# A four-layer encoder on one core: the last combination of each down group split in parts, other work moved behind its neighbours

## The chip, the cores and the metric

The kernel runs on one core of a Trainium2 chip. The metric is the device time of one execution in microseconds (us). The core has five engines that run their own queues of instructions: TensorE (PE, matrix products), VectorE (DVE), ScalarE (ACT), GpSimd (POOL) and SyncE (SP, which here only issues DMAs). They wait for each other on semaphores.

## The reference

An encoder trunk of four layers on x of 512 tokens by 1024 features, all in float32. Each layer has a token mixer and a gated feed-forward part with a short convolution:

```python
def rmsnorm(x, g):
    y = x * lax.rsqrt(jnp.mean(x * x, axis=-1, keepdims=True) + EPS)
    return y * g

def conv_ffn(h, w_up, dw_w, dw_b, w_down):
    u = dwconv(h @ w_up, dw_w, dw_b)          # 1024 -> 5632, 3 taps
    val, gate = jnp.split(u, 2, axis=-1)
    return (jax.nn.gelu(gate) * val) @ w_down # 2816 -> 1024

def reference(x, ...):
    for i in range(4):
        h = rmsnorm(x, norm1_g[i])
        x = x + mixer(h)     # 0, 3: convolution module, 1: attention, 2: retention
        h = rmsnorm(x, norm2_g[i])
        x = x + conv_ffn(h, ffn_w_up[i], ffn_dw_w[i], ffn_dw_b[i], ffn_w_down[i])
    return x
```

The mixer of layer 1 is a neighbourhood attention with 16 heads of 64: queries and keys are normalised per head, each token attends to a window of the grid of 8 by 64 tokens, and a bias by relative position is added. The padding outside a window is kept out by a mask.

## The kernel before

x stands transposed in SBUF, as eight tiles of 128 features by 512 tokens. A float32 product is made of three matmuls: every operand is split into a high part (a cast to the matmul's type) and a low part (what the cast left), and high by high, high by low and low by high are summed (`mm3`, L181 to L184, and `mm3s`, L186 to L189). A weight tile is loaded by SP into one of two raw buffers (L159), its high part is cast on ACT (`wh`, L168) and its low part subtracted on DVE (`wl`, L169); there are three buffers each. `load_w_acc` (L172) makes the low part in another way: ACT writes the cast (L176) and the negated cast (L177), and a DMA of POOL's queue adds the raw weight onto the latter (L178). The list `ACC` says which up tiles n do so; their products with the low part come as one block of eight matmuls at the tile's end (L317). `split` (L191) is the same for activations: a cast on ACT (L192), a subtraction on DVE (L193).

**Feed-forward.** The up product has 44 tiles of 128 columns, taken in pairs j (value tile n = 2j and gate tile n = 2j + 1, 22 pairs). `up` (L305) does one tile. For the pairs in `UPS[l]` the pair is done by `up_macro`, which makes seven products of half size from sums of weights and sums of inputs (as in Strassen's scheme); the sums of inputs, `ch` and `cl`, are made by `combos(p)` at j = 4 to 7. The norm's scale is applied late: until `scale_rest` has split the scaled x into `xhi`, `xlo`, products use unscaled x and `mid` scales their results.

`mid(j)` (L395) takes a pair's results, does the three taps and the gelu, and writes the product into a tile F of seven 256-column blocks: blocks 1 to 3 get two pairs' results (L427), and blocks 4, 5 (L430), 0 (L432) and 6 (L433) are sums of these. `split(F, hi, lo)` then makes Hh and Hl of all 1792 columns in one cast and one subtraction. Pairs from 16 on are multiplied plainly (`down_rest`). For the others the down product is done in two groups of four such tiles (`PARTS`), again by seven products per output column block, with blocks 1, 6, 0, 4, 5, 2, 3 in this order; `weights` (L479) builds the weight sums that this needs: `wh`, `wl` of the raw tile and of ws, then an addition into ws (L485) and its split h, l, an addition into wq (L489) and its split h, l. The first products of a group leave out the last tile p, which is taken as soon as it is there. Partial results are added onto x in DRAM (`xd`); x is spilled there at the layer's start.

**Attention.** Its start is the column norm (`stats1`, L275): a column sum, a root by three Newton steps of small operations on DVE (`rsqrt`, L195 to L205), and `rstd_col`, which scales the projected queries and keys. `mask` is loaded on ACT's queue and POOL adds it to the bias tiles (`bm`, L950). `qz` are tiles whose unused half is zero; a memset and four copies on DVE write the zeros (L856, L860). POOL squares (L889) and scales (L903) queries and keys, whose per-head norms go through `rsqrt` on DVE with 16 columns.

**What sets the order.** The program is written in one order, and a scheduler, which has a model of durations, decides the order on each engine; `behind(name)` and `issue_after` make instructions come after a named one. On the engine the order is then fixed: an instruction that waits holds up what is behind it.

Of the kernel before, what the change touches and what calls it, by code (L numbers as in the profile page):

```python
# [9 lines left out]
F32R = mybir.dt.float32r  # L10
I32 = mybir.dt.int32
AF = mybir.ActivationFunctionType
# [5 lines left out]
P = 128  # L18
T = 512
# [5 lines left out]
FT = 22  # L25
# [54 lines left out]
LATEW = True  # L80
ACC = tuple(n for n in range(3, 2 * FT, 2) if n // 2 not in (8, 9, 16, 17))


@with_exitstack
def tile_trunk(
# [17 lines left out]
    def nm(s):  # L103
        uid[0] += 1
        return f"{s}{uid[0]}"
# [85 lines left out]
    def split(src, hi, lo, n=None):  # L191
        state["cast"] = nc.scalar.copy(hi, src)  # L192
        return nc.vector.tensor_tensor(lo, src, hi.bitcast(F32), SUB)  # L193
# [81 lines left out]
    def stats1(ps=None):  # L275
        ps = bank(psb) if ps is None else ps
        c = colsum(sqacc, ps)
        v = sm(4)
        nc.vector.tensor_scalar(v, c, 1.0 / D, EPS, MUL, ADD)
        r = rsqrt(v, 4)  # L280
        nc.vector.tensor_copy(rstd_col, r)

# [16 lines left out]
    def ffn(l, after):  # L299
        with ExitStack() as st:  # L300
# [3 lines left out]
            def up(n):  # L304
                c = n // 2 + FT * (n % 2)  # L305
                ps = bank(psa)
                acc = n in ACC
                wh, wl = load_w_acc(f_up[l, c], D) if acc else load_w(f_up[l, c], D)
                for k in range(KD):
                    s = slice(k * P, (k + 1) * P)  # L310
                    if acc:
                        nc.tensor.matmul(ps, wh[:, s], xhi[k], start=k == 0, stop=False)  # L312
                        nc.tensor.matmul(ps, wh[:, s], xlo[k], start=False, stop=False)  # L313
                    else:
                        mm3(ps, wh[:, s], wl[:, s], xhi[k], xlo[k], k == 0, k == KD - 1)
                for k in range(KD if acc else 0):
                    nc.tensor.matmul(ps, wl[:, k * P:(k + 1) * P], xhi[k], start=False, stop=k == KD - 1)  # L317
                if n == 3 and l == 1:
                    stats1(state["spare"])
                if n == S2[l]:  # L320
                    stats2()
                    scale_first()
                if n == SCALED[l] - 1:
                    scale_rest()
                return ps

            def scale_first():
# [4 lines left out]
            def scale_rest():  # L332
                for k in range(KD):
                    split(x[k], xhi[k], xlo[k])

            ch, cl = {}, {}

            def combos(p):
                e, o = x[2 * p], x[2 * p + 1]
                c = hp.tile([P, D], F32, tag="ws", name=nm("cx"), bufs=NWS)  # L340
                q = [c[:, i * 256:(i + 1) * 256] for i in range(4)]
                nc.vector.tensor_tensor(q[0], e[:, 256:], e[:, :256], SUB)
                nc.vector.tensor_tensor(q[1], o[:, :256], e[:, :256], SUB)
                nc.vector.scalar_tensor_tensor(q[2], o[:, :256], -1.0, q[0], MUL, SUB)
# [50 lines left out]
            def mid(j, pv, pg):  # L395
# [32 lines left out]
                if j % 2 == 0:  # L428
                    return
                nc.vector.tensor_tensor(  # L430
                    F[:, 4:6, :], F[:, 1:3, :], F[:, :1, :].broadcast_to([P, 2, 256]), SUB)
                nc.vector.scalar_tensor_tensor(F[:, 0, :], F[:, 2, :], -1.0, F[:, 4, :], MUL, SUB)  # L432
                nc.vector.scalar_tensor_tensor(F[:, 6, :], F[:, 0, :], -1.0, F[:, 3, :], MUL, SUB)  # L433
                hi = hp.tile([P, 7, 256], F32R, tag=f"Hh{p % SLOT_H}", name=nm("Hh"))
                lo = hp.tile([P, 7, 256], F32R, tag=f"Hl{p % SLOT_H}", name=nm("Hl"))
                split(F, hi, lo)
                H[p] = (hi, lo)
# [146 lines left out]
            ups = up_first()  # L584
            for k in range(KD):
                nc.sync.dma_start(xd[k], x[k])
            done, n = 0, 2
# [25 lines left out]

            starts = {2 * p1 + (l == 1 and q == 0): q for q, (_, p1) in enumerate(PARTS)}
            for j in range(1, FT):
# [228 lines left out]
    def nat(after):  # L844
        PER = 4
        with ExitStack() as st:
# [3 lines left out]
            mask = np1.tile([P, 3, 256], F32, tag="mask", name=nm("mask"))  # L850
            nc.scalar.dma_start(mask, nmask.rearrange("p (v k) -> p v k", v=3))
            kstart = (0, 64, 192, 256)
            qzs = [[np1.tile([P, 2, T], F32R, tag=f"qz{n}{i}", name=nm("qz")) for i in range(2)]
                   for n in range(NQZ)]
            zz = np1.tile([P, 1], F32, tag="zz", name=nm("zz"))
            nc.vector.memset(zz, 0.0)  # L856
            for qz in qzs:
                for i in range(2):
                    zp = slice(64 - 64 * i, 128 - 64 * i)
                    nc.vector.tensor_copy(qz[i][zp], zz[zp].unsqueeze(2).broadcast_to([64, 2, T]))  # L860

# [15 lines left out]
            def proj(g):  # L877
                qk = np2.tile([P, 2, 4, 256], F32, tag="qk", name=nm("qk"), bufs=NQK)
                for part in range(2):
                    pss = part_proj(g, part)  # L880
                    with hp():
                        ss = np2.tile([P, 16], F32, tag="ss", name=nm("ss"))
                        for tb in range(4):
                            nc.scalar.activation(qk[:, part, tb, :], pss[tb], AF.Copy,
                                                 scale=rstd_col[:, tb:tb + 1])
                        for t2 in range(2):
# [115 lines left out]

            def att(g, qk, va, vs):
                if PRE:
                    pre = [att_prep(g, pi, qk) for pi in range(2)]
                    return [att_pair(g, pi, *pre[pi], va, vs) for pi in range(2)]
                return [att_pair(g, pi, *att_prep(g, pi, qk), va, vs) for pi in range(2)]
# [481 lines left out]
```

## Time and profile before

| | us |
|---|---|
| executions (3) | 2546.81, 2550.06, 2555.11 |
| median | 2550.06 |
| profiled execution | 2551.38 |
| its span, first to last instruction | 2549.5 |
| PE busy in it | 2516.3 (99%) |
| DVE, ACT, POOL busy | 1831.9, 1266.3, 387.1 |

The profile comes from one execution. Its views are a page of totals, lists of groups of instructions, lists of waits (who waited for what, how long in total, how often, the longest), and timelines. A timeline row has the start in us, the duration, the engine, the line of the kernel, the operation, the tile written and the tiles read, their shapes, the count, and in brackets how long the engine had been idle and what ended that. Matmuls overlap each other: of 512 columns they start 0.23 us apart at full clock, of 256 columns 0.12. "Granted clock" is PE's clock as a share of full speed.

### The profile page before, as it was taken

What the parts mean: (1) busy time and instruction counts of PE and PEld (TensorE: products, weight loads), DVE (VectorE), ACT (ScalarE), POOL (GpSimd) and SP (SyncE); (2) the same over time, 40 slices, a digit from 0 to 9 for tenths busy, and PEclk for the clock granted to TensorE, in tenths of its full rate; (3) what the DMA queues carried; (4) which work ended last, traced back from release to release, by engine and by line L of the source; (5) the groups of instructions that cost most, each with busy time, mean ns of one, the idle gap of its engine ahead of it and who ended that gap; (6) DMA issues with size and microseconds to landing.
All of it is one profiled execution on the core that took longest, in us unless ns stands there. A gap on an engine that the chain in (4) does not pass through costs nothing.

```text
span 2549.5 us, 38773 instructions
## 1 busy us (share of the span) xinstructions
PE 2516.3 (99%) x15166; PEld 2174.0 (85%) x15166; DVE 1831.9 (72%) x3004; ACT 1266.3 (50%) x1763; POOL 387.1 (15%) x476
## 2 busy tenths in 40 slices
PE   9999999999999999999999999999999999999999
PEld 7888898989998888898888888789898887789897
DVE  7976867677877785768566565687777887686765
ACT  5454645564656554555332323464545445464543
POOL 1214110103421201120000000211011121201010
PEclk9999999999999999999999999999999999999999
DMA  7736776743233566674222222467674672577674
GB/s 243 233 92 181 192 167 170 163 142 105 86 89 108 139 179 154 176 181 125 83 75 67 91 70 71 139 175 165 168 171 139 200 224 89 135 188 162 175 162 141
DMA packets 124041, 370.70 MB, mean 145 GB/s; under 512 B 15136, under 2 KB 18080, under 8 KB 123856
## 3 DMA queue, kind: packets, MB, share of 16 engines
q1 hardware_dynamic: 90816, 277.30, 34.8%
q0 software_dynamic: 31744, 88.19, 18.6%
q10 hardware_dynamic: 1296, 2.72, 0.3%
q8 instruction: 119, 1.95, 0.3%
q14 instruction: 66, 0.54, 0.1%
HBM read 333.59 MB, written 30.79 MB: 143 GB/s over the span
## 4 chain that ended last, share of the span: by engine, by line
PE 86%; DVE 5%; DMA 4%; ACT 3%; issue 2%; DVEq 0%; ACTq 0%; POOL 0%; SPq 0%; POOLq 0%
PE ps L182 21%; PE ps L183 21%; PE ps L184 21%; PE ps L317 3%; PE ps L313 3%; PE ps L312 3%; PE ps L188 3%; PE ps L187 3%; PE ps L189 3%; DMA wr<-in_f_down 3%; DVE wl L169 1%; PE ps L749 1%; PE ps L748 1%; PE ps L747 1%; ACT wh L168 1%
## 5 line engine op out<-in xcount | busy, mean ns | idle before, releaser
L168 ACT CAST wh<-wr 128x1024 fp32r<-128x1024 f32 (+1 forms) x310 | 317.9, 1028 | 557.9 <-PE ps L183 280.1
L169 DVE TENSOR_TENSOR wl<-wr,wh 128x1024 fp32r<-128x1024 f32 (+1 forms) x307 | 370.9, 1208 | 185.7 <-ACT wh L168 169.3
L183 PE MATMUL ps<-xl,wh 128*128 128x512 f32 (+1 forms) x1248 | 487.6, 391 | 0.3 <-DVE xl L254 0.3
L182 PE MATMUL ps<-xh,wh 128*128 128x512 f32 (+1 forms) x1248 | 485.6, 390 | 1.1 <-ACT wh L168 0.6
L184 PE MATMUL ps<-xh,wl 128*128 128x512 f32 (+1 forms) x1248 | 485.6, 390 | 0.1
L182 PEld LDWEIGHTS ps<-xh,wh 128*128 128x128 f32 x1248 | 234.9, 188 | 55.0 <-ACT wh L168 1.5
L184 PEld LDWEIGHTS ps<-xh,wl 128*128 128x128 f32 x1248 | 234.8, 188 | 52.9 <-DVE wl L169 0.5
L183 PEld LDWEIGHTS ps<-xl,wh 128*128 128x128 f32 x1248 | 234.9, 188 | 52.4 <-DVE xl L254 0.6
L182 PE MATMUL ps<-Hh,wh 128*128 128x256 f32 (+1 forms) x734 | 219.1, 308 | 5.1 <-ACT wh L168 5.0
L183 PE MATMUL ps<-Hl,wh 128*128 128x256 f32 (+1 forms) x734 | 222.3, 307 | 0.8 <-DVE Hl L193 0.8
L184 PE MATMUL ps<-Hh,wl 128*128 128x256 f32 (+1 forms) x734 | 220.5, 307 | 0.3
L312 PE MATMUL ps<-xh,wh 128*128 128x512 f32 x416 | 164.6, 396 | 1.3 <-ACT wh L176 1.3
L313 PE MATMUL ps<-xl,wh 128*128 128x512 f32 x416 | 164.4, 395 | 0.0
L188 PE MATMUL ps<-wl,xh 128*128 128x256 f32 (+1 forms) x512 | 159.7, 313 | 1.8 <-DVE wl L169 1.8
L187 PE MATMUL ps<-wh,xh 128*128 128x256 f32 (+1 forms) x512 | 159.8, 315 | 1.1 <-ACT xh L251 1.1
L189 PE MATMUL ps<-wh,xl 128*128 128x256 f32 (+1 forms) x512 | 159.9, 313 | 0.0
L182 PEld LDWEIGHTS ps<-Hh,wh 128*128 128x128 f32 x734 | 136.9, 188 | 16.2 <-ACT wh L168 8.7
L183 PEld LDWEIGHTS ps<-Hl,wh 128*128 128x128 f32 x734 | 137.8, 188 | 8.3 <-DVE Hl L193 1.0
L184 PEld LDWEIGHTS ps<-Hh,wl 128*128 128x128 f32 x734 | 137.0, 188 | 9.0 <-DVE wl L169 2.1
L178 POOL DMA_DIRECT2D wl<-in_f_up x52 | 46.6, 897 | 463.0 <-ACT wl L177 349.7
L317 PE MATMUL ps<-xh,wl 128*128 128x512 f32 x416 | 107.4, 400 | 4.6 <-DMA wl<-in_f_up 4.6
L182 PE MATMUL ps<-Hh,h 128*128 128x256 f32 x384 | 108.6, 283 | 0.0
(330 smaller groups left out, 6182.2 us busy)
## 6 DMA issues: line engine op xcount, KB each, us to landing
wr<-in_f_up SPq DMA_DIRECT2D x144, 512.0 KB, 4.0
wraw<-in_cdw SPq DMA_DIRECT2D x56, 608.0 KB, 5.2
wl<-in_f_up POOLq DMA_DIRECT2D x52, 512.0 KB, 7.7
ws<-in_f_down SPq DMA_DIRECT2D x32, 512.0 KB, 7.3
wr<-in_f_down SPq DMA_DIRECT2D x32, 512.0 KB, 6.9
ws<-in_f_down POOLq DMA_DIRECT2D x32, 512.0 KB, 8.4
xd<-t POOLq DMA_DIRECT2D x64, 256.0 KB, 5.8
wr<-in_cw_in SPq DMA_DIRECT2D x30, 512.0 KB, 4.1
```

What stands on the lines that cost most here:

```text
L168: nc.scalar.copy(hi[:, :n], raw[:, :n])
L169: eng.tensor_tensor(lo[:, :n], raw[:, :n], hi[:, :n].bitcast(F32), SUB)
L178: nc.gpsimd.dma_start(lo[:, :n], src.bitcast(F32R), accum_op=ADD)
L182: nc.tensor.matmul(o, wh, ah, start=first, stop=False, skip_group_check=free)
L183: nc.tensor.matmul(o, wh, al, start=False, stop=False, skip_group_check=free)
L184: nc.tensor.matmul(o, wl, ah, start=False, stop=last, skip_group_check=free)
L187: nc.tensor.matmul(o, ah, wh, start=first, stop=False)
L188: nc.tensor.matmul(o, ah, wl, start=False, stop=False)
L189: nc.tensor.matmul(o, al, wh, start=False, stop=last)
L312: nc.tensor.matmul(ps, wh[:, s], xhi[k], start=k == 0, stop=False)
L313: nc.tensor.matmul(ps, wh[:, s], xlo[k], start=False, stop=False)
L317: nc.tensor.matmul(ps, wl[:, k * P:(k + 1) * P], xhi[k], start=False, stop=k == KD - 1)
```

## The change

It has five pieces.

1. `ACC` loses the tiles n with n // 2 = 10. In layers 0, 2 and 3 pair 10 is a macro, so only n = 21 of layer 1 changes: it is loaded by `load_w`.
2. The spill of x to `xd` is emitted in `up` at n = 2 (`SPILL`) and no longer after `up_first`.
3. The first two subtractions of `combos` are put behind the last split of `scale_rest` (`state["scaled"]`).
4. Where a tile F is the last of a down group, its split is done in three parts: blocks 1 to 3 before the combinations L430 to L433, then blocks 4 to 6, then block 0.
5. In the attention, the mask's DMA is issued behind the last scaling of the queries and keys of g = 0 (`state["qk"]`), and the zeros of `qz` are put behind the copy into `rstd_col` (`state["stat"]`). `COVER` is (0, 0) and adds nothing to `starts`.

In the new kernel line numbers are higher by 2 to 17 (the copy at L168 is L170, the cast at L192 is L194, L489 is L504, L950 is L966).

ACT at the entry of layer 0's second down group, before and then changed (Hh is the cast of F, ws and wq the weight sums, wr the raw weight of the next step):

```order
L168 CAST wh_4513<-ws_4485 128x1024
L192 CAST h_4518<-ws_4485 128x512
L192 CAST Hh_4503<-F_4421 128x1792
L192 CAST h_4523<-wq_4486 128x1024
L168 CAST wh_4603<-wr_4601 128x1024
L530 COPY t_4529<-ps_4527 128x256
```

```order
L170 CAST wh_4521<-ws_4489 128x1024
L194 CAST Hh_4504<-F_4425 128x768
L194 CAST Hh_4504<-F_4425 128x256
L194 CAST h_4526<-ws_4489 128x512
L194 CAST Hh_4504<-F_4425 128x768
L170 CAST wh_4611<-wr_4609 128x1024
L194 CAST h_4531<-wq_4490 128x1024
L545 COPY t_4537<-ps_4535 128x256
```

The one cast of F has become three, the first of them ahead of the cast of ws, and the cast of the next weight (`wh`) now stands ahead of that of wq.

DVE in layer 1 around up tile n = 21, before and then changed (wl_10813 and wl_10824 are the low part of the same weight, that of macro 11; l_10476 and l_10488, l_10596 and l_10608, wq_10575 and wq_10587 are the same tiles likewise):

```order
L489 TENSOR_TENSOR wq_10455<-ws_10454,wq_10455 128x512
L516 TENSOR_TENSOR t_10361<-ps_10360,t_10361 128x512
L539 TENSOR_TENSOR t_10544<-t_10544,ps_10480 128x512
L193 TENSOR_TENSOR l_10476<-wq_10455,h_10475 128x1024
L169 TENSOR_TENSOR wl_10813<-wr_10810,wh_10812 128x1024
L489 TENSOR_TENSOR wq_10575<-ws_10574,wq_10575 128x512
L516 TENSOR_TENSOR t_10481<-ps_10480,t_10481 128x512
L169 TENSOR_TENSOR wl_10817<-ws_10711,wh_10816 128x1024
```

```order
L195 TENSOR_TENSOR l_10488<-wq_10467,h_10487 128x1024
L504 TENSOR_TENSOR wq_10587<-ws_10586,wq_10587 128x512
L531 TENSOR_TENSOR t_10493<-ps_10492,t_10493 128x512
L195 TENSOR_TENSOR l_10608<-wq_10587,h_10607 128x1024
L171 TENSOR_TENSOR wl_10824<-wr_10821,wh_10823 128x1024
L171 TENSOR_TENSOR wl_10828<-ws_10723,wh_10827 128x1024
L554 TENSOR_TENSOR t_10676<-t_10676,ps_10612 128x512
```

The low part for macro 11 stood ahead of the addition into wq; it now stands behind it and behind the low part that is made of it.

POOL at the same place, before and then changed:

```order
L475 DMA ws_10805<-in_f_us 128x1024
L540 DMA xd_115<-t_10544 128x512
L178 DMA wl_10751<-in_f_up 128x1024
L517 DMA xd_116<-t_10481 128x512
L540 DMA xd_117<-t_10664 128x512
```

```order
L490 DMA ws_10816<-in_f_us 128x1024
L532 DMA xd_114<-t_10373 128x512
L555 DMA xd_115<-t_10556 128x512
L532 DMA xd_116<-t_10493 128x512
L555 DMA xd_117<-t_10676 128x512
```

The accumulating load for n = 21 (wl_10751) is gone, and the load of the next weight sum stands one transfer of results further ahead.

POOL at the start of the attention, before and then changed (t are the squares):

```order
L178 DMA wl_5430<-in_f_up 128x1024
L950 TENSOR_TENSOR bm_6278<-W_6276,mask_5782 128x256 x3
L950 TENSOR_TENSOR bm_6284<-W_6282,mask_5782 128x256 x3
L889 TENSOR_TENSOR t_5939<-qk_5794 128x512
L889 TENSOR_TENSOR t_5942<-qk_5794 128x512
L889 TENSOR_TENSOR t_6085<-qk_5794 128x512
L903 TENSOR_TENSOR qk_5794<-qk_5794,sm_5966 128x512 x2
L889 TENSOR_TENSOR t_6088<-qk_5794 128x512
L903 TENSOR_TENSOR qk_5794<-qk_5794,sm_6110 128x512 x2
```

```order
L180 DMA wl_5438<-in_f_up 128x1024
L905 TENSOR_TENSOR t_5941<-qk_5796 128x512
L905 TENSOR_TENSOR t_5944<-qk_5796 128x512
L905 TENSOR_TENSOR t_6087<-qk_5796 128x512
L919 TENSOR_TENSOR qk_5796<-qk_5796,sm_5968 128x512 x2
L905 TENSOR_TENSOR t_6090<-qk_5796 128x512
L966 TENSOR_TENSOR bm_6286<-W_6284,mask_5790 128x256 x3
L966 TENSOR_TENSOR bm_6292<-W_6290,mask_5790 128x256 x3
L919 TENSOR_TENSOR qk_5796<-qk_5796,sm_6112 128x512 x2
```

The six bias sums, which read the mask, stood ahead of all work on queries and keys; they now stand between the last square and the second scaling.

The diff:

```diff
--- before.py
+++ after.py
@@ -78,7 +78,9 @@
 UPS = ((10, 11, 18, 19), (11, 12, 18, 19), (10, 11, 18, 19), (10, 11, 18, 19))
 COMBO = (4,5,6,7)
 LATEW = True
-ACC = tuple(n for n in range(3, 2 * FT, 2) if n // 2 not in (8, 9, 16, 17))
+COVER = (0, 0)
+SPILL = 2
+ACC = tuple(n for n in range(3, 2 * FT, 2) if n // 2 not in (8, 9, 10, 16, 17))
 
 
 @with_exitstack
@@ -278,7 +280,7 @@
         v = sm(4)
         nc.vector.tensor_scalar(v, c, 1.0 / D, EPS, MUL, ADD)
         r = rsqrt(v, 4)
-        nc.vector.tensor_copy(rstd_col, r)
+        state["stat"] = nc.vector.tensor_copy(rstd_col, r)
 
     def stats2(phased=None):
         ps = bank(psb)
@@ -317,6 +319,8 @@
                     nc.tensor.matmul(ps, wl[:, k * P:(k + 1) * P], xhi[k], start=False, stop=k == KD - 1)
                 if n == 3 and l == 1:
                     stats1(state["spare"])
+                if n == SPILL:
+                    spill()
                 if n == S2[l]:
                     stats2()
                     scale_first()
@@ -324,6 +328,10 @@
                     scale_rest()
                 return ps
 
+            def spill():
+                for k in range(KD):
+                    nc.sync.dma_start(xd[k], x[k])
+
             def scale_first():
                 for k in range(KD):
                     nc.vector.scalar_tensor_tensor(
@@ -331,7 +339,7 @@
 
             def scale_rest():
                 for k in range(KD):
-                    split(x[k], xhi[k], xlo[k])
+                    state["scaled"] = split(x[k], xhi[k], xlo[k])
 
             ch, cl = {}, {}
 
@@ -339,8 +347,9 @@
                 e, o = x[2 * p], x[2 * p + 1]
                 c = hp.tile([P, D], F32, tag="ws", name=nm("cx"), bufs=NWS)
                 q = [c[:, i * 256:(i + 1) * 256] for i in range(4)]
-                nc.vector.tensor_tensor(q[0], e[:, 256:], e[:, :256], SUB)
-                nc.vector.tensor_tensor(q[1], o[:, :256], e[:, :256], SUB)
+                with behind("scaled"):
+                    nc.vector.tensor_tensor(q[0], e[:, 256:], e[:, :256], SUB)
+                    nc.vector.tensor_tensor(q[1], o[:, :256], e[:, :256], SUB)
                 nc.vector.scalar_tensor_tensor(q[2], o[:, :256], -1.0, q[0], MUL, SUB)
                 nc.vector.scalar_tensor_tensor(q[3], q[2], -1.0, o[:, 256:], MUL, SUB)
                 cl[p] = hp.tile([P, D], F32R, tag=f"cl{p}", name=nm("cl"))
@@ -427,13 +436,19 @@
                 nc.vector.tensor_tensor(F[:, b:b + 2, :].rearrange("p a b -> p (a b)"), acc[0], acc[1], MUL)
                 if j % 2 == 0:
                     return
+                hi = hp.tile([P, 7, 256], F32R, tag=f"Hh{p % SLOT_H}", name=nm("Hh"))
+                lo = hp.tile([P, 7, 256], F32R, tag=f"Hl{p % SLOT_H}", name=nm("Hl"))
+                if p + 1 in (p1 for _, p1 in PARTS):
+                    split(F[:, 1:4, :], hi[:, 1:4, :], lo[:, 1:4, :])
                 nc.vector.tensor_tensor(
                     F[:, 4:6, :], F[:, 1:3, :], F[:, :1, :].broadcast_to([P, 2, 256]), SUB)
                 nc.vector.scalar_tensor_tensor(F[:, 0, :], F[:, 2, :], -1.0, F[:, 4, :], MUL, SUB)
                 nc.vector.scalar_tensor_tensor(F[:, 6, :], F[:, 0, :], -1.0, F[:, 3, :], MUL, SUB)
-                hi = hp.tile([P, 7, 256], F32R, tag=f"Hh{p % SLOT_H}", name=nm("Hh"))
-                lo = hp.tile([P, 7, 256], F32R, tag=f"Hl{p % SLOT_H}", name=nm("Hl"))
-                split(F, hi, lo)
+                if p + 1 in (p1 for _, p1 in PARTS):
+                    for c in (slice(4, 7), slice(0, 1)):
+                        split(F[:, c, :], hi[:, c, :], lo[:, c, :])
+                else:
+                    split(F, hi, lo)
                 H[p] = (hi, lo)
 
             def up_first():
@@ -582,8 +597,8 @@
                     after(o)
 
             ups = up_first()
-            for k in range(KD):
-                nc.sync.dma_start(xd[k], x[k])
+            if SPILL == 0:
+                spill()
             done, n = 0, 2
 
             def mids(upto):
@@ -611,7 +626,7 @@
                     if COMBO[p] == j:
                         combos(p)
 
-            starts = {2 * p1 + (l == 1 and q == 0): q for q, (_, p1) in enumerate(PARTS)}
+            starts = {2 * p1 + (l == 1 and q == 0) + COVER[q]: q for q, (_, p1) in enumerate(PARTS)}
             for j in range(1, FT):
                 ups_of(j)
                 w0 = down_sums(0, starts[j], state["load"]) if j in starts else None
@@ -848,16 +863,17 @@
             np1 = st.enter_context(tc.tile_pool(name=nm("nat"), bufs=1, reuse_waits=RW))
             np2 = st.enter_context(tc.tile_pool(name=nm("nat2"), bufs=2, reuse_waits=RW))
             mask = np1.tile([P, 3, 256], F32, tag="mask", name=nm("mask"))
-            nc.scalar.dma_start(mask, nmask.rearrange("p (v k) -> p v k", v=3))
             kstart = (0, 64, 192, 256)
             qzs = [[np1.tile([P, 2, T], F32R, tag=f"qz{n}{i}", name=nm("qz")) for i in range(2)]
                    for n in range(NQZ)]
             zz = np1.tile([P, 1], F32, tag="zz", name=nm("zz"))
-            nc.vector.memset(zz, 0.0)
-            for qz in qzs:
-                for i in range(2):
-                    zp = slice(64 - 64 * i, 128 - 64 * i)
-                    nc.vector.tensor_copy(qz[i][zp], zz[zp].unsqueeze(2).broadcast_to([64, 2, T]))
+
+            def zeros():
+                nc.vector.memset(zz, 0.0)
+                for qz in qzs:
+                    for i in range(2):
+                        zp = slice(64 - 64 * i, 128 - 64 * i)
+                        nc.vector.tensor_copy(qz[i][zp], zz[zp].unsqueeze(2).broadcast_to([64, 2, T]))
 
             def part_proj(g, part):
                 pss = [bank(psa), bank(psa)]
@@ -881,8 +897,8 @@
                     with hp():
                         ss = np2.tile([P, 16], F32, tag="ss", name=nm("ss"))
                         for tb in range(4):
-                            nc.scalar.activation(qk[:, part, tb, :], pss[tb], AF.Copy,
-                                                 scale=rstd_col[:, tb:tb + 1])
+                            state["qk"] = nc.scalar.activation(qk[:, part, tb, :], pss[tb], AF.Copy,
+                                                               scale=rstd_col[:, tb:tb + 1])
                         for t2 in range(2):
                             sqt = t512()
                             z = qk[:, part, 2 * t2:2 * t2 + 2, :]
@@ -1001,6 +1017,11 @@
                 return S[:64, :256]
 
             def att(g, qk, va, vs):
+                if g == 0:
+                    with tc.issue_after(state["qk"].ins):
+                        nc.scalar.dma_start(mask, nmask.rearrange("p (v k) -> p v k", v=3))
+                    with behind("stat"):
+                        zeros()
                 if PRE:
                     pre = [att_prep(g, pi, qk) for pi in range(2)]
                     return [att_pair(g, pi, *pre[pi], va, vs) for pi in range(2)]
```

## The prediction

> **What bounds the kernel now.** I read the page's first part, then the waits of PE, then the busy time and granted clock of single stretches, and last the timeline around the three places that the change touches.
>
> ```profile
> span 2549.5 us, 38773 instructions
> PE 2516.3 (99%) x15166; PEld 2174.0 (85%) x15166; DVE 1831.9 (72%) x3004; ACT 1266.3 (50%) x1763; POOL 387.1 (15%) x476
> ```
>
> The matmuls are the bound: PE is idle for 2549.5 − 2516.3 = 33 us. The change takes no matmul away, so it can only win what PE loses in waits, and what a wait does to the clock behind it. The waits concerned:
>
> ```profile
> PE ps L182 <- ACT wh L168: 5.6, 8, 1.4
> PE ps L317 <- DMA wl<-in_f_up: 4.6, 1, 4.6
> PE ps L188 <- DVE wl L169: 1.8, 1, 1.8
> PE ps L183 <- DVE Hl L193: 0.8, 1, 0.8
> PE ps L183 <- DVE xl L254: 0.3, 1, 0.3
> ```
>
> Columns are total us, number of waits, longest. The first and the fourth lie, but for two short ones, where a down group begins; the second is one accumulated weight of layer 1; the third is the start of the attention; the last is a low part of x. A wait costs more than its own length if the clock falls behind it (columns of the next view: stretch, its length, PE, PEld, DVE, ACT, POOL, granted clock, DMA share, GB/s):
>
> ```profile
> 585.20:588.80 3.60, 3.60 (x20) 3.60 (x20) 1.40 (x3) 1.57 (x4) 1.94 (x2) 0.53 0.79 233
> 993.00:997.00 4.00, 4.00 (x13) 3.32 (x12) 0.72 (x1) 0.00 (x0) 0.00 (x0) 0.50 0.58 185
> 997.00:1000.00 3.00, 3.00 (x22) 3.00 (x21) 2.52 (x5) 0.90 (x2) 0.00 (x0) 0.77 0.00 0
> ```
>
> PE counts as busy in these stretches, yet does less: behind the attention wait 3.6 × (1 − 0.53) = 1.7 us are lost, behind the layer-1 wait 4 × 0.50 + 3 × 0.23 = 2.7 us.
>
> The page on the clock gate, "TensorE: Matmul & The Clock Gate" (section "What's actually happening") in the Trainium skill, has the clock fall to half after about 3.4 us of idleness. Here a single wait of 1.84 us was followed by a halved stretch, so by that rule the 1.7 us behind the attention would have another cause and stay, and the sum below would be 1.7 smaller. The trace speaks against the threshold and for the halving.
>
> **Layer 1, up tile n = 21 (ACC).** Before: ACT writes the negated high part, a POOL DMA adds the raw weight to it, and PE runs the low products as one block at the end.
>
> ```profile
> 987.44 0.39 PE L313 MATMUL ps<-xl,wh 128*128 128x512 f32 x1
> 992.41 1.65 PE L317 MATMUL ps<-xh,wl 128*128 128x512 f32 x3 [4.57 <-DMA wl<-in_f_up]
> 981.90 1.59 POOL L178 DMA_DIRECT2D wl<-in_f_up  x1
> wl<-in_f_up POOLq DMA_DIRECT2D x1, 512.0 KB, 10.5
> 979.31 1.23 DVE L169 TENSOR_TENSOR wl<-wr,wh 128x1024 fp32r<-128x1024 f32 x1 [2.08 <-ACT wh L168]
> 983.52 0.69 DVE L489 TENSOR_TENSOR wq<-ws,wq 128x512 f32<-128x512 f32 x1 [2.99 <-DMA wq<-in_f_down]
> 988.32 1.22 DVE L193 TENSOR_TENSOR l<-wq,h 128x1024 fp32r<-128x1024 f32 x1
> ```
>
> The DMA goes out at 981.90 and takes 10.5 us, 4.6 more than PE has. Now one subtraction of 1.23 us on DVE makes the low part; its raw tile and its cast are there several microseconds before PE comes to n = 21 (the cast stood at 972 to 974 before the negated copy), so this wait and its clock loss go: 4.6 + 2.7 = 7.3. What is added is DVE work in a row that is kept in order. In the new order the low part of the following macro's weight (wl_10824) no longer runs ahead of the addition at L489, which waits for its own DMA until 983.5; behind that addition stand a low part of 1.2 us, one PE eviction, and then wl_10824. Counting on from 983.5 through the cast of h, it is ready about 989.3, while PE, without its stall, comes to it about 988.4: 1 us. The s2 low part behind it is some 1 us late by the same row, an earlier low part (l_10488) about 0.4. So 7.3 − 2.4 = **4.9**. Bounds: 7.3 if PE's fillers cover all three, 3 if each of them is twice as late.
>
> **Start of the attention (mask, zeros).**
>
> ```profile
> 574.59 2.79 DVE L860 CAST qz<-zz 64x1024 fp32r<-64x1024 f32 x4
> 578.25 4.23 POOL L950 TENSOR_TENSOR bm<-W,mask 128x256 f32<-128x256 f32 x6 [57.01 <-DMA mask<-in_nmask]
> 577.72 0.69 DVE L224 TENSOR_REDUCE sm<-ps 128x4 f32<-128x512 f32 x1 [0.33 <-PE ps L222]
> 580.45 0.65 DVE L202 SCALAR_TENSOR_TENSOR sm<-sm 128x4 f32<-128x4 f32 x1
> 582.53 0.16 DVE L202 SCALAR_TENSOR_TENSOR sm<-sm 128x4 f32<-128x4 f32 x1
> 583.40 1.23 DVE L169 TENSOR_TENSOR wl<-wr,wh 128x1024 fp32r<-128x1024 f32 x1
> 584.68 0.39 PE L188 MATMUL ps<-wl,xh 128*128 128x256 f32 x1 [1.84 <-DVE wl L169]
> ```
>
> The small operations of the norm's root take 0.65 us each while POOL's six bias sums run and 0.16 us once they end at 582.48. Six of them are slowed, by 6 × 0.5 = 3 us, and the low part of the weight for which PE waits 1.84 us stands in the same row. With the sums elsewhere it starts some 2.4 us earlier, at about 581.0, and is ready at 582.2, before PE comes to it at 582.8. The zeros are not what costs here: the reduction behind them waits for PE at 577.72, after their end. So 1.84 and the 1.7 of the clock go: 3.5.
>
> The sums do not vanish. The mask is now issued behind the last scaling of g = 0's keys, on ACT's queue, and POOL has the sums between the two halves of the qk work:
>
> ```profile
> mask<-in_nmask ACTq DMA_DIRECT2D x1, 384.0 KB, 3.5
> 596.35 0.84 ACT L884 ACTIVATE qk<-ps,rstd_col 128x256 f32<-128x256 f32 x2 [0.37 <-PE ps L189]
> 603.66 2.05 POOL L903 TENSOR_TENSOR qk<-qk,sm 128x512 f32<-128x512 f32 x2 [3.37 <-DVE sm L205]
> 607.68 0.71 PE L927 MATMUL ps<-ident,qk 128*128 128x128 f32 x5
> ```
>
> That scaling ends at 597.2, and 3.5 earlier now: 593.7. The mask lands 3.5 later, 597.2; six sums take 4.23, to 601.4. The key's root on DVE, thirteen operations of 128x16, is slowed meanwhile, as above, and ends about 602.9; the scaling of 2.05 ends about 605.0 to 606.2. PE transposes its result at 607.68 before, 604.1 now: a new wait of 1 to 2 us, taken as 1.5. The zeros, 2.79 us on DVE behind the norm, push the first square sums back by about 1 us; the rest of that chain has idle time for it. Sum: 3.5 − 1.5 = **2.0**. Bounds: 3.5 if fillers hide the new wait; −0.5 if it is 2.3 and draws a halved stretch of 1.7 after it.
>
> A rule that bears on this is in the Trainium skill's "SBUF — State Buffer" ("Who interferes with whom"): two-input VectorE operations and GpSimd shut each other out. The 0.65 against 0.16 agrees with it, each small operation lasting about as long as one of the six sums (4.23 / 6 = 0.70). By it the 1.23 us low parts of the next weights would lose time too when they meet the moved sums; that is within the 1.5.
>
> **Entry of the eight down groups (split in three).**
>
> ```profile
> 438.16 0.62 ACT L192 CAST h<-ws 128x512 fp32r<-128x512 f32 x1 [2.62 <-DVE ws L485]
> 438.69 1.69 ACT L192 CAST Hh<-F 128x1792 fp32r<-128x1792 f32 x1
> 441.22 1.04 ACT L168 CAST wh<-wr 128x1024 fp32r<-128x1024 f32 x1
> 440.41 2.02 DVE L193 TENSOR_TENSOR Hl<-F,Hh 128x1792 fp32r<-128x1792 f32 x1 [0.74 <-ACT Hh L192]
> 440.03 0.28 PE L184 MATMUL ps<-Hh,wl 128*128 128x256 f32 x1
> 440.43 0.50 PE L182 MATMUL ps<-Hh,wh 128*128 128x256 f32 x2
> 442.31 0.39 PE L182 MATMUL ps<-Hh,wh 128*128 128x256 f32 x1 [1.38 <-ACT wh L168]
> ```
>
> This is layer 0's second group. PE lacks the high part until 440.4, then a weight until 442.26, with the low part of H ready at 442.43; from 440.03 to 442.31 three matmuls ran that take 0.12 each, so 2.28 − 0.36 = 1.9 us are lost. In the new order ACT, idle for 2.62 us ahead of 438.16, casts the first 768 columns there, and DVE subtracts them before the sums of the weights. From casts of 512, 1024 and 1792 columns (0.62, 1.04, 1.69) one of 768 takes 0.83; the subtraction, by 1792 at 2.02 and 1024 at 1.22, 0.95. DVE's row then puts the last combination (L433) at 438.9 to 439.3, ACT the cast for ws to 439.6, the last 768 columns to 440.4, and the weight, now ahead of wq's cast, to 441.4 where it was 442.26. The last subtraction ends about 441.8. Gain 0.9 of 1.9. The extra two casts (0.4 us of ACT) and two subtractions (0.3 of DVE) lie where these engines are idle.
>
> The other groups have the same build with smaller waits. The waits of PE, asked for the stretch around each entry (groups 0.0, 1.1, 2.0, 2.1 and 3.1 by layer and group; 1.0 is the 0.8 for Hl above, 0.1 the 1.4, 3.0 has none):
>
> ```profile
> PE ps L182 <- ACT wh L168: 0.2, 1, 0.2
> PE ps L182 <- ACT wh L168: 0.7, 1, 0.7
> PE ps L182 <- ACT wh L168: 1.0, 1, 1.0
> PE ps L182 <- ACT wh L168: 0.8, 1, 0.8
> PE ps L182 <- ACT wh L168: 0.9, 1, 0.9
> ```
>
> That is 5.8 over seven waits. Scaled as here (1.9 lost for a wait of 1.4) about 8 us are lost at all entries. A gain of 0.9, or the whole wait where it is shorter, gives 0.2 + 0.9 + 0.8 + 0.7 + 0.9 + 0.8 + 0.9 = **5.2**. Bounds: 8 if all is won, 1 if the next operand comes as late.
>
> **The rest.** The spill of x moves in the program but on SP's queue it stands where it stood: 0. The input combinations move behind the eight low parts of x, six subtractions on DVE; their products are used first by the Strassen-like macro products from j = 10, and PE's only wait on a low part of x is 0.3 us: 0, ±0.5. The order of PE in the attention changes beyond the start; I take 0, ±1.5.
>
> **Sum.** 4.9 + 2.0 + 5.2 = 12.1 against the profiled execution's 2551.4 (span 2549.5 and 1.9 around it): 2539.3. That execution is 1.3 above the median of the runs shown, so **2538 us** against 2550.06.
>
> **Rivals.**
> 1. *The down groups' wait only changes hands.* For it: weight (442.26) and low part (442.43) become ready within 0.2 us of each other, so a later one is close behind; and ACT's cast for ws is itself 0.8 us later in the new row. Against it: both casts and subtractions found idle time ahead. Then C gives 1 in place of 5.2: 2542.
> 2. *Layer 1 pays in DVE's row.* For it: three low parts stand behind an addition that waits for its own DMA, and a wait there may draw the halved clock again. Then 7.3 is given back but for about 0: 2543. Against it: PE has some products of earlier groups in between.
> 3. *Slower: the moved mask is late.* POOL runs in order, so everything that the mask holds up holds up the scaling of the keys, and PE's transposes behind it. With a landing as slow as the weight's above, 10.5 instead of 3.5, sums end at 608.4, the scaling at 610.5, PE waits 6.4 and loses 2.7 of clock: 9.1, less the 3.5 won, so 5.6 lost, and the rest of the sum still wins: 2545.5. It decides for slower only when the mask needs about 23 us: 18.6 of wait + 2.7 − 3.5 − 4.9 − 5.2 = 7.7, 2558. Against it: the queues carried 3.5 us for this transfer at a DMA share of 0.8, and it goes out in a stretch that is no busier.
> 4. *The change does nothing for PE* (the halved stretches come at such times anyway, and waits move): 2549 to 2551. Against it: the 4.6 us wait has a cause that is taken away outright.
>
> **Chances and range.** Forecast 0.70, first rival 0.10, second 0.10, third 0.04, fourth 0.06. Executions of the kernel before differ by 0.3%, 7.7 us, and less than that can't be told from no change; the border is 2542.4. The forecast's own range, from the bounds of the terms, is 2533 to 2543 at most; all bounds won give 2550 − 7.3 − 3.5 − 8 = 2531, all lost 2550 − 3 + 0.5 − 1 = 2546.5. The range is 2531 to 2546, which leaves out the third and the fourth rival and some of the tails. Faster: most of the forecast (0.66), half of the first rival and some of the second, 0.75. Within: 0.21. Slower: 0.04.
>
> **What would show it.** The wait on the accumulated weight (4.6) is gone from PE's list, and no wait over 1.5 has come near 985 to 1000; clock 1.00 there. The wait of 1.8 for the low part at the attention is gone, and the small operations there take 0.16; a wait of 1 to 2 us stands before the transposes. The wait on wh at L168 falls from 5.6 to about 1 to 2, with Hl not above 1. It is wrong if PE's total of waits falls by less than 6, or if a halved stretch appears at a new place.

## The result, and the profile after

| | median us | span of the profiled execution |
|---|---|---|
| before | 2548.98 | 2549.5 |
| changed | 2543.11 | 2542.8 |

The ratio is 0.9976 with a 95% interval of 0.9968 to 0.9984: 6.1 us less, at most 8.2. The forecast was 2538, with a range of 2531 to 2546. The sign and the range held, but the gain is half of the one forecast, and less than the 0.3% that the prediction called noticeable. The interval, from fourteen executions of each kernel, leaves out no change.

The page's first rows and the waits of PE in the changed kernel (columns as before: total us, number, longest):

```profile
span 2542.8 us, 38815 instructions
PE 2513.8 (99%) x15166; PEld 2172.5 (85%) x15166; DVE 1831.1 (72%) x3021; ACT 1268.5 (50%) x1778; POOL 389.5 (15%) x475
...
PE ps L186 <- DVE wl L171: 4.3, 3, 2.0
...
PE ps L184 <- ACT wh L170: 2.7, 5, 0.7
...
PE ps L943 <- POOL qk L919: 1.6, 2, 1.2
PE ps L314 <- ACT wh L178: 1.6, 1, 1.6
...
PE ps L184 <- DVE t L554: 0.9, 2, 0.5
...
PE ps L185 <- DVE Hl L195: 0.4, 1, 0.4
```

The 4.6 us on the accumulated weight are gone and so are the 1.8 us at the attention; the waits on `wh` fell from 5.6 to 2.7. New are a row that was forecast (POOL's scaling, 1.6) and one that was feared (low parts of weights, 4.3 in three waits). Two more are new and were not thought of. The 1.6 at L314 is a single wait in layer 1, at 1003.9: the cast in front of it (`wh`, L178) waited for its raw weight's DMA until 1002.80. The 0.9 at L554 are two waits for result banks. PE's waits add up to 29.1 us before and 24.6 changed, so they fell by 4.5.

What each place cost PE can be added up from the starts of the matmuls. Each matmul adds the time to the next start, less the usual time for its shape; this takes in waits and slow clock alike. In us, from the two profiled executions:

| place | before | changed | won |
|---|---|---|---|
| layer 0, both down entries | 2.5 | 0.9 | 1.6 |
| attention, to about 650 | 6.6 | 2.7 | 3.9 |
| layer 1, feed-forward from 940 to 1130 | 10.0 | 12.9 | −2.9 |
| layer 2, two entries and one up tile | 3.2 | 0 | 3.2 |
| layer 3, entries and one up tile | 2.1 | 1.2 | 0.9 |
| sum | 24.4 | 17.7 | 6.7 |

6.7 is the difference of the spans. Layer 1 was to win 6.4 (4.9 at n = 21 and 1.5 at its entries) and lost 2.9. The other four places were to win 5.7 and won 9.6. In layer 3 that is not the split's doing: its entries lose 1.2 before (at 2419) and 1.2 changed (at 2286), and the 0.9 is the up tile's, which piece 3 was not expected to touch.

Layer 1's 12.9 are 4.1 at n = 21 (984 to 990), 1.8 at the wait of 1003.9, 2.2 at the second group's entry (1.0 before), 3.7 at 1108 to 1126, and the rest at result banks.

**An entry that went well.** ACT, DVE and PE at layer 0's second down group, timeline of the changed kernel:

```profile
434.91 0.83 ACT L194 CAST Hh<-F 128x768 fp32r<-128x768 f32 x1
437.02 0.41 ACT L194 CAST Hh<-F 128x256 fp32r<-128x256 f32 x1 [1.28 <-DVE F L445]
439.02 0.83 ACT L194 CAST Hh<-F 128x768 fp32r<-128x768 f32 x1
439.75 1.04 ACT L170 CAST wh<-wr 128x1024 fp32r<-128x1024 f32 x1
440.25 0.95 DVE L195 TENSOR_TENSOR Hl<-F,Hh 128x768 fp32r<-128x768 f32 x1
440.85 0.39 PE L184 MATMUL ps<-Hh,wh 128*128 128x256 f32 x1 [0.56 <-ACT wh L170]
```

The parts take 0.83 and 0.95 us as estimated, the first lies in time in which ACT had been idle before, and the wait of 1.38 us has become one of 0.56.

**The attention.** The norm's root, the weight behind it, the sums at their new place and PE's transposes, timeline of the changed kernel:

```profile
577.30 0.16 DVE L204 SCALAR_TENSOR_TENSOR sm<-sm 128x4 f32<-128x4 f32 x1
579.33 1.22 DVE L171 TENSOR_TENSOR wl<-wr,wh 128x1024 fp32r<-128x1024 f32 x1 [0.48 <-ACT wh L170]
595.77 4.21 POOL L966 TENSOR_TENSOR bm<-W,mask 128x256 f32<-128x256 f32 x6
599.36 0.66 DVE L205 TENSOR_TENSOR sm<-sm,sm 128x16 f32<-128x16 f32 x1
600.05 0.18 DVE L207 SCALAR_TENSOR_TENSOR sm<-sm,sm 128x16 f32<-128x16 f32 x1
601.63 3.35 POOL L919 TENSOR_TENSOR qk<-qk,sm 128x512 f32<-128x512 f32 x2 [1.65 <-DVE sm L207]
605.03 0.98 PE L943 MATMUL ps<-ident,qk 128*128 128x128 f32 x7 [1.22 <-POOL qk L919]
```

The small operations of the norm's root take 0.15 to 0.17 us now. The key's root took over the slow ones (0.66 until 600.0, 0.18 after), as reckoned, and PE pays two waits, 1.6 us together.

**Layer 1.** DVE and PE around n = 21, timeline of the changed kernel; then DVE's waits for wq between 960 and 1005, changed and before; then what the queue of SP waited for before it issued wq's transfer (L491), changed kernel, 955 to 985; then the granted clock behind PE's wait:

```profile
981.51 0.69 DVE L504 TENSOR_TENSOR wq<-ws,wq 128x512 f32<-128x512 f32 x1 [8.28 <-DMA wq<-in_f_down]
983.46 1.23 DVE L195 TENSOR_TENSOR l<-wq,h 128x1024 fp32r<-128x1024 f32 x1 [0.65 <-ACT h L194]
984.60 1.22 DVE L171 TENSOR_TENSOR wl<-wr,wh 128x1024 fp32r<-128x1024 f32 x1
985.87 0.38 PE L186 MATMUL ps<-xh,wl 128*128 128x256 f32 x1 [1.97 <-DVE wl L171]
```
```profile
DVE wq L504 <- DMA wq<-in_f_down: 10.7, 2, 8.3
```
```profile
DVE wq L489 <- DMA wq<-in_f_down: 7.2, 2, 4.2
```
```profile
SPq L491 <- DVE l L195: 12.3, 3, 7.1
```
```profile
986.80:990.20 3.40, 3.05 (x15) 2.76 (x14) 3.40 (x7) 0.95 (x2) 0.88 (x1) 0.50 0.44 78
```

DVE stands for 8.3 us in front of the addition into wq, then makes up its row, and the macro weight's low part behind it comes 2 us late; half the clock follows. The transfer for which DVE stands went out at 973.3, when DVE had split the previous wq (972.02 to 973.24): there is one buffer. The second group has the same step: DVE stands 7.8 us in front of the addition and PE waits 1.48 us at 1109.94. A further wait for a low part, 0.89, stands at 1126.16.

### The profile page after: what moved, and what is told of

It is laid out like the page before. It is cut to its first block, busy times and chain, and to the rows that moved or that the text cites. A ratio compares the mean times of both kernels' runs of the same rounds, so it can differ in the third digit from the quotient of the medians.

```text
span 2542.8 us, 38815 instructions
## 1 busy us (share of the span) xinstructions
PE 2513.8 (99%) x15166; PEld 2172.5 (85%) x15166; DVE 1831.1 (72%) x3021; ACT 1268.5 (50%) x1778; POOL 389.5 (15%) x475
## 4 chain that ended last, share of the span: by engine, by line
PE 90%; DVE 4%; DMA 3%; ACT 2%; issue 1%; POOL 0%; DVEq 0%; SPq 0%; ACTq 0%; POOLq 0%
PE ps L184 21%; PE ps L186 21%; PE ps L185 21%; PE ps L314 4%; PE ps L315 4%; PE ps L319 4%; PE ps L189 3%; PE ps L191 3%; PE ps L190 3%; DMA wr<-in_f_down 1%; PE ps L764 1%; PE ps L763 1%; PE ps L762 1%; DVE wl L171 1%; PE ps L470 1%
## 5 line engine op out<-in xcount | busy, mean ns | idle before, releaser
L170 ACT CAST wh<-wr 128x1024 fp32r<-128x1024 f32 (+1 forms) x311 | 319.0, 1027 | 559.3 <-PE ps L185 261.4
L314 PE MATMUL ps<-xh,wh 128*128 128x512 f32 x408 | 161.5, 396 | 1.6 <-ACT wh L178 1.6
L186 PE MATMUL ps<-Hh,l 128*128 128x256 f32 x384 | 108.9, 284 | 0.1
```

Of the source, the lines that this page charges most:

```text
L170: nc.scalar.copy(hi[:, :n], raw[:, :n])
L186: nc.tensor.matmul(o, wl, ah, start=False, stop=last, skip_group_check=free)
```

## The experiments

Times are given by the ratio of a kernel's executions to those of the kernel before, times 2549 us; two experiments have one execution each and are read by their profile. "Layer 1" is the loss of PE in one profiled execution from 940 to 1130, added up as in the table above (before 10.0, changed 12.9). Piece 2, the spill, has no run of its own; on SP's queue its eight issues start at 182.5 to 209.6 before and at 182.3 to 209.4 changed, so it stands where it stood.

### The parts alone

The split alone (the kernel before with piece 4):

> The kernel before with the split of the last combination alone. Forecast of the prediction: 5.2 less than before (2544). By the changed kernel's profile, layer 0 won 1.6, layers 2 and 3 about 2.3 to 4; with layer 1 undisturbed 4 to 6 less: 2543 to 2545. Rival (the wait only changes hands): 1 less, 2548.

Ratio 0.9966 (0.9954 to 0.9979): 8.7 us less (5.4 to 11.7), more than either forecast. Layer 1: 8.2.

The plain load of n = 21 alone:

```diff
-ACC = tuple(n for n in range(3, 2 * FT, 2) if n // 2 not in (8, 9, 16, 17))
+ACC = tuple(n for n in range(3, 2 * FT, 2) if n // 2 not in (8, 9, 10, 16, 17))
```

> The kernel before with the plain load of n = 21 alone. Order theory: the wait and its clock go and nothing comes for it, 6 to 7.5 less: 2541.5 to 2543. Prediction's term: 4.9 less, 2544. Rival (plain loading brings DVE's row late by itself): 0 to 3 less, 2546 to 2549.

Ratio 0.9992 (0.9983 to 1.0001): 2 us less, not told from nothing. Layer 1: 6.8; the 7.5 us at n = 21 are gone, but waits on weights stand elsewhere. PE's waits from 930 to 1165:

```profile
PE ps L184 <- DVE wl L169: 1.9, 2, 1.2
PE ps L182 <- ACT wh L168: 1.2, 1, 1.2
PE ps L183 <- DVE Hl L193: 0.7, 1, 0.7
```

In the same profile 3.8 us were lost at layer 3's first entry, where the execution of before lost nothing, though the edit touches no weight there. The four other experiments without the split lost 1.1 to 2.3 at that entry too, so the loss does not come from the plain load; why the execution of before has none is open. The order theory's 2541.5 to 2543 is missed, and so is the prediction's 4.9 less: the time is the rival's. In layer 1, 4.0 were lost at the second entry with the slower clock, 1.0 before. Whether the plain load brought that is not shown: a wait of 1.2 stands there too in the experiment with piece 3 alone, which keeps the old load.

The moved mask and zeros alone (piece 5):

> The kernel before with the moved mask and zeros alone. Prediction's term: 2.0 less (2547). By the changed kernel's profile: 3.6 won at 583 to 589, 2.3 won at 622 to 647, 2.05 paid at 602 to 606, so 3.9 less: 2545. Rival (the new wait draws a slower clock and eats it): 2549.

Ratio 0.9989 (0.9979 to 0.9999): 2.8 us less (0.3 to 5.4), between the two forecasts. In the profile the wait at 584 and the ones at 622 to 647 are gone, and PE's only wait from 575 to 680 is the new one:

```profile
PE ps L942 <- POOL qk L918: 1.6, 2, 1.2
```

The input combinations behind the splits alone (piece 3):

> The kernel before with the input combinations behind the input's splits alone. Prediction's term: 0 (2549). By the changed kernel's profile: the two waits on ACT's cast of an accumulated weight in layers 2 and 3 (0.9 each with the slower starts) go, 1.9 less: 2547.

Ratio 0.9998 (0.9989 to 1.0007): no difference that can be told; both forecasts, 0 and 1.9 us less, lie within the interval. In the profile two waits of the kernel before are gone; this row of it has no counterpart:

```profile
PE ps L312 <- ACT wh L176: 1.3, 2, 0.7
```

They were worth 1.9 us with their slower starts; the entries lost 1.5 more than before in that execution. So the piece removes two waits, and what it is worth stays open (at most 2.8 us less by the interval).

What follows: 8.7 + 2.0 + 2.8 + 0.5 = 14 us by the parts, 6.1 together. Nearly 8 us are lost in the parts' meeting; each part's interval reaches 2 to 3 us to either side, so that sum may be off by some 5.

### Which parts don't go together

The changed kernel with layer 1 left unsplit, and the changed kernel with n = 21 loaded in the old way:

```diff
-                if p + 1 in (p1 for _, p1 in PARTS):
+                if l != 1 and p + 1 in (p1 for _, p1 in PARTS):
```
```diff
-ACC = tuple(n for n in range(3, 2 * FT, 2) if n // 2 not in (8, 9, 10, 16, 17))
+ACC = tuple(n for n in range(3, 2 * FT, 2) if n // 2 not in (8, 9, 16, 17))
```

> The changed kernel with the last split of a down group left in one piece in layer 1 only. Order theory (the plain load of n = 21 and the split in layer 1 together make the scheduler put a macro weight's low part behind the addition into wq, and PE waits there): the stalls of layer 1 between 984 and 1004 (5.9 us with their slower clock) and between 1108 and 1126 (3.7) go, two small entry waits (1 each) come back; 2533 to 2536. Rival (plain loading in itself brings wq late): those stalls stay, 2541 to 2545.

> The changed kernel with n = 21 of layer 1 loaded in the old, accumulating way. Order theory: the old wait (4.6 and 2.7 of clock) is back, but the waits on low parts at 1108 to 1126 are gone; 2538 to 2542. Rival (the split in itself makes these late waits): they stay, 2545 to 2548.

Ratios 0.9955 (0.9943 to 0.9968) and 0.9956 (0.9943 to 0.9968): 11 us less than before each, and 5 less than the changed kernel, which has both (the intervals just touch). Layer 1: 7.8 and 6.2. With the accumulating load the old wait is back, but smaller, and it is PE's only one from 930 to 1165:

```profile
PE ps L319 <- DMA wl<-in_f_up: 3.4, 1, 3.4
```

With layer 1 unsplit the stalls at 984 to 990 and 1108 to 1126 are gone, but the order theory's 2533 to 2536 is missed. The entries wait 1.2 each, and this row of PE's waits from 930 to 1165 stays:

```profile
PE ps L186 <- DVE wl L171: 2.6, 2, 1.9
```

Its 1.9 is at 1001: the low part of that weight stands behind the unsplit subtraction of Hl (2.02 us at 997.11), and half the clock follows from 1001.2.

So the plain load and the split, each of which lowers layer 1's loss alone (6.8 and 8.2 against 10.0), cost each other's gain there. In DVE's order the macro weight's low part stands behind the addition into wq and behind that sum's split in both groups when both pieces are there; with one of them it stands ahead of the addition in both groups, and in the kernel before ahead of it in the first group and ahead of the split in the second.

### Is it the order, or what the order waits for?

Four buffers for low parts, by which the low part stands ahead of the addition again; and two buffers for wq, by which it stays behind, but the transfer goes out earlier:

```diff
-    wlo = ctx.enter_context(tc.tile_pool(name="wlo", bufs=3))
+    wlo = ctx.enter_context(tc.tile_pool(name="wlo", bufs=4))
```
```diff
-                sg = hp.tile([P, D], F32, tag="wq", name=nm("wq"))
+                sg = hp.tile([P, D], F32, tag="wq", name=nm("wq"), bufs=2)
```

> The changed kernel with four buffers for low parts of weights where it has three, by which the scheduler puts the macro weight's low part ahead of the addition into wq again. Order theory: in layer 1 the stalls at 984 to 1004 and 1108 to 1126 (9.6 us with their clock) lose 6 or more; 2534 to 2538. Rival (the weights themselves land late, whatever the order): 2541 to 2545.

> The changed kernel with two buffers for the weight sum wq, so that its transfer no longer waits until the previous sum is split. The macro weight's low part stays behind the addition into wq, but that addition should not wait for a transfer. If the transfer behind the order is the cause: the same stalls go, 2533 to 2538. If the order alone costs (the engine's row is too long): 2541 to 2545.

Four buffers: 0.9977 (0.9968 to 0.9985), no better than the changed kernel. Layer 1 falls to 9.1, 4 less and not 6, and waits on accumulated weights at three places elsewhere, which were not there, cost 3.9. The order theory in its first form falls. DVE and PE near n = 21 there:

```profile
982.17 0.69 DVE L504 TENSOR_TENSOR wq<-ws,wq 128x512 f32<-128x512 f32 x1 [7.33 <-DMA wq<-in_f_down]
984.11 1.23 DVE L195 TENSOR_TENSOR l<-wq,h 128x1024 fp32r<-128x1024 f32 x1 [0.65 <-ACT h L194]
986.38 0.68 DVE L554 TENSOR_TENSOR t<-t,ps 128x512 f32<-128x512 f32 x1
```
```profile
987.12 0.39 PE L184 MATMUL ps<-Hh,h 128*128 128x256 f32 x1 [2.24 <-DVE t L554]
```

DVE still stands 7.3 us before the addition. The low part is past it now, but the next thing behind it that PE needs, the freeing of a result bank (L554), is as late: 2.24 us in place of 1.97. Without a halved stretch behind it this costs 2.5 and not 4.1; one does follow another late low part, 1.7 us at 1003.4, and that costs 4.0.

Two buffers for wq: 0.9968 (0.9959 to 0.9978), 8.2 less than before, which is between the two forecasts. Layer 1: 2.7, with one wait left from 930 to 1165. In the other layers the same edit moved the order for the worse; PE's waits there on the cast of F, which the changed kernel does not have:

```profile
PE ps L184 <- ACT Hh L194: 4.0, 5, 1.5
```

So the buffer of wq is the cause in layer 1: its transfer can't start until the previous wq is split, and all that stands behind the addition in DVE's row waits with it. With the second buffer the addition also stands further ahead in DVE's row; how much each of the two gives is not shown.

### The buffer where it helps

The second buffer in layer 1 only (`bufs=2 if l == 1 else 1`), with the plain and with the accumulating load of n = 21:

> The changed kernel with the second wq buffer in layer 1 only. If the transfer of wq is what blocks DVE's row there, layer 1's losses fall from 13.5 us to about 4 and the other layers stay as in the changed kernel: 2532 to 2535. If the gain of two buffers came from other layers: 2538 to 2541.

> The same with n = 21 of layer 1 loaded in the old, accumulating way. If the plain load is worth something once wq is out of the way: slower than with it by 3 to 7 us, 2537 to 2540. If the wait on the accumulation was itself a consequence of wq (POOL's row behind a late weight sum): the same time, 2532 to 2535.

2533.96 us, ratio 0.9940 (0.9926 to 0.9954), and 2537.26, 0.9955 (0.9942 to 0.9967). Layer 1: 2.6 and 7.1. Both times are where the first forecast of each put them. The first is the fastest kernel of this study, 15 us below before. The transfer of the group's last wq goes out at 956.6 in it, where the changed kernel issued it at 973.3. Its waits of DVE for wq from 940 to 990, and of PE from 930 to 1165:

```profile
DVE wq L504 <- DMA wq<-in_f_down: 0.5, 1, 0.5
...
PE ps L184 <- ACT wh L170: 0.7, 1, 0.7
```

With wq out of the way the plain load is worth 3.3 us, and no execution of the one kernel is as fast as any of the other; the 2.7 us wait on the accumulation stays with the old load, so it is not a consequence of wq.

### Mask or zeros

The two halves of piece 5, each alone:

> The kernel before with the mask's transfer moved and the zeros left where they were. Prediction: the wait at 584.7 (1.84) is gone and the new one before the transposes (1.6) is there, as when both are moved; the zeros are not on the path. Rival (the zeros cost): a wait for the low part stays, 1 us or more.

> The kernel before with the zeros moved behind the norm and the mask left where it was. Prediction: the wait at 584.7 stays at 1.8, the small operations there take 0.65 us, no new wait before the transposes. Rival (the zeros cost): the wait is gone.

One execution each, 2541.97 and 2546.95. PE's waits from 575 to 680, first with the mask moved alone, then with the zeros moved alone:

```profile
PE ps L944 <- POOL qk L920: 1.1, 1, 1.1
```
```profile
PE ps L190 <- DVE wl L171: 1.9, 1, 1.9
PE ps L1005 <- DVE e L1003: 0.9, 3, 0.4
```

The zeros are not on the path: with them moved alone the waits of before are still there, and with the mask moved alone the new wait is 0.5 us shorter than with both. The three small waits at 622 to 647 belong to the mask too.

## Why the prediction was right and wrong

**Right in its sign, its range and the mechanism of two of three terms; the range by luck in part.** Layer 1 came out 9.3 worse than forecast (−2.9 for 6.4), and the other places 3.9 better (9.6 for 5.7), for causes of which most were not foreseen. By its own signs the prediction was wrong: PE's total of waits fell by 4.5 where less than 6 was to show it wrong, and a wait of 1.97 with a halved stretch behind it came at 985.87, where no wait over 1.5 and a clock of 1.00 were to be.

*Attention, 2.0 forecast.* 2.8 measured alone. The wait of 1.84 went, a new one of 1.6 came (1.5 forecast), in the place and for the reason given. Not seen were the waits on the softmax's scaling at 622 to 647, worth 2.3 with slower starts. They went with the mask's move; how is not shown, since POOL's bias sums still run there in the changed kernel (from 619.32 and from 636.50). And the 1.7 of slow clock, counted in full, are not in every execution. So the size of this term is luck in part.

*Down groups, 5.2 forecast.* 8.7 (5.4 to 11.7) alone, so the mechanism was right and the term too small; the entries lost 8.0 before and 1.4 in that profile, 6.6 won. At layer 0's second entry the parts' durations were those reckoned, and the weight was ready at 440.8 where 441.4 was forecast, in an execution that the first entry's gain has put 0.5 ahead. The gain was capped at 0.9 for each entry, where whole losses with their slow starts went. The 6.6 lies within the interval. In the two profiles the spans differ by 10.9, and nearly all of the rest is that the execution before had halved clock stretches at 134.8, 585.3 and 2124.8, outside the feed-forward parts, and the execution with the split has none there.

*First rival, the wait only changes hands:* it did not; with the split alone no entry lost more than 0.8 us. *Third, a late mask:* the sums began at 595.77, earlier than reckoned. *Fourth, nothing for PE:* excluded by the interval.

**Wrong: the term for n = 21, 4.9.** The step that failed is "counting on from 983.5", the arrival of wq's transfer in the trace of before, whose place in time I took as fixed while PE moved ahead. In the changed kernel PE is 5.5 us ahead there, so that arrival had to be at 978.0 for the reckoned 1 us; it was at 981.4, and the wait was 1.97 and drew the half clock. Of this lateness 2.0 are the transfer, which was 8.2 us under way where it had been 6.2 (why is not shown), and 1.5 its issue: in both kernels it waits for the split of the previous wq, and that came 4.0 earlier (973.3 for 977.3) and not 5.5. The second failed step is in the same sentence: I looked at one group, and the order has the same row in the second (3.7 us at 1108 to 1126). This is the second rival, "layer 1 pays in DVE's row", which put the time at 2543 and got 10 in 100; the mechanism that it named, low parts behind an addition that waits for its own DMA, is what the two buffers for wq took away. Its size was too small: it put layer 1's term for n = 21 at about 0, and the layer gave back 9.3. That its 2543 is also the time measured is luck, by what the other places won beyond the forecast.

*The combinations, 0 forecast:* two waits of 0.66 us in layers 2 and 3 went, which the prediction does not mention; too small to be told by the time.

## What to carry to other kernels

When an edit removes a stall in front of an in-order engine's row, everything later comes earlier except the transfers, whose release may hang on a buffer; look for the instruction of that row that waits for a transfer, and for what PE needs behind it, in every group that repeats the pattern. Two good edits can spoil each other through the order that a scheduler makes of them: compare the order of both together with that of each alone. And reordering behind such a wait here only changed which operand was late (1.97 us for a low part, 2.24 for a result bank); the second buffer ended it.

## What the runs showed of the hardware

A short stall can cost its length again in clock, by where it falls. Within an execution the clock's records change on a fixed grid of 3.41 us. In the fourteen profiles, 26 stretches of that grid had PE idle for 1.85 us or more, and every one was followed by a stretch at half clock. Of the stretches at full clock none was with 1.33 us or less; between these it went both ways. Stretches that were themselves at half clock are another matter: four had 0.6 to 1.6 us of idleness and were followed by a second one. The same wait at the attention's start shows what the grid does: before, 1.84 us, all within one stretch and followed by a granted clock of 0.53 (shown in the prediction); with the zeros alone moved, 1.87 us, of which 1.62 fell into one stretch, and the clock stayed at 1.00:

```profile
583.09 0.39 PE L190 MATMUL ps<-wl,xh 128*128 128x256 f32 x1 [1.87 <-DVE wl L171]
```
```profile
583.30:586.70 3.40, 3.40 (x30) 3.40 (x30) 3.32 (x6) 1.57 (x4) 1.43 (x2) 1.00 0.53 189
```

By the Trainium skill ("TensorE: Matmul & The Clock Gate", "What's actually happening") the clock falls after a window of about 3.4 us without work; here somewhat over half a window was enough. The measurement decides, and the part of the prediction that took the slow stretch as sure should have taken it as a chance.

VectorE's plain subtractions suffer from GpSimd too, not only the small operations: the low parts of 1.22 us took 1.97 and 1.80 while the late scaling ran in the changed kernel, and that scaling 3.35 where it was 2.05.

```profile
602.11 1.97 DVE L171 TENSOR_TENSOR wl<-wr,wh 128x1024 fp32r<-128x1024 f32 x1
604.26 1.80 DVE L171 TENSOR_TENSOR wl<-wr,wh 128x1024 fp32r<-128x1024 f32 x1 [0.18 <-ACT wh L170]
```
